# Four idle products ahead of the first large one, and the samples' heads at full width of the array

## The chip, the cores and the metric

The kernel runs on one core of a Trainium2 chip. The metric is the device time of one execution in microseconds (us). The engines are TensorE (PE; its weight loads are shown as PEld), VectorE (DVE), ScalarE (ACT), GpSimd (POOL) and SyncE (SP), which issues most DMAs. Each engine works through its own queue in order and waits on semaphores for the others.

## What is computed

The reference is one inference step of a hybrid decoder layer, for a prompt of 1024 tokens and for 8 samples of 4 tokens each, with a width of 1024. Cut to what matters here:

```
h, gate = adaln_in(x, c, w_ada, b_ada, g_norm)
(mq, mk, mv, mi, mf, mo, mz, aq, ak, av, az, gm, ga) = split_in(h @ w_in)
y_m, C, n, m = mlstm_branch(mq, mk, mv, mi, mf, mo, mz, C0, n0, m0, ...)
...                                  # windowed attention gives y_a
u = sigmoid(gm) * (y_m @ w_mo) + sigmoid(ga) * (y_a @ w_ao)
x = x + gate * (u @ w_o)             # then a last RMSNorm
```

The mLSTM branch has 4 heads of 128 channels. For the samples, a head takes its 32 tokens together:

```
s   = (q k^T) * exp(dmat - m_hat)        # 32 x 32, zero between samples
num = s v + w_inter * (q C)              # C: one 128 x 128 matrix a sample
C_new = decay * C + sum_s w_end k_s v_s^T
```

## The kernel before

Activations are kept with channels on the 128 partitions and tokens in columns. Large matrix products take each operand as a high and a low part in fp32r and add three products of the parts (h_h with wh, h_h with wl, h_l with wh). Small products and transpositions are plain f32; one of these is carried out as two passes (a transposition as one). The rows of the profile show a pass as rows * columns of the array that its weights take (128*128, 128*32, 32*32) and the size of its output.

TensorE's order is fixed by the program: `in_order` ties each product or transposition to the one before it, and `mm` and `tr` record them (L275 and L280). DVE and ACT are tied in the same way (class `Ordered`, L220) only in the first stage and the last one; from `V.on = S.on = False` on, a scheduler places their instructions by what they depend on. POOL is placed by the scheduler from the start. Every tile comes from a pool; a new tile of a tag waits until the tile whose buffer it takes over has been read for the last time. PSUM has four tags with two buffers each: `pg`, `pa`, `pb` and `po`.

**The first stage.** `warm(11)` issues eleven products of a tile of ones into a `pb` tile that nobody reads. Sums of squares of x follow as the loads of x land, then `ada_halves(adas[0])`: the first of the adaLN rows (`ada_q`), copied by ACT and turned by small products (`adat_q`) into columns in two `pb` tiles. ACT and DVE make the scales A and B from them, ACT makes h_h of the first two channel blocks, POOL casts the first weights (wh_ak, wh_av), DVE makes the low parts. The loop over `two` then runs `pair`, the large products for keys and values (`g_ak`, `g_av`), with the row sums for the second half (`xb`), more `ada_q` chunks and gate products in between.

**The middle.** `block_products` runs the input projections in pairs of 128 columns as seven block products each (Strassen's form with Winograd's sums): twelve passes of 512 columns into one of the banks bx, bw, by and bz. Between the passes `side.tick()` lets streams of smaller work issue a step: the prompt's heads (`head`, stream m), attention, weights for the last stage (`out_weights`, stream g: wor, wosh, wosl) and the samples' heads (`sample_head`, stream s). A planner's clock in the program (`side.now`) decides when a step may come; it counts product sizes and lags.

**A sample's head.** `qs`, `ks` and `vs` hold the samples' q, k and v for all heads, [128, 4, 32] each. `sample_head(h)` transposes the 32 columns of k and of v (tile stk), multiplies k and q into sS, forms `et` (a sum of `sxb` and the mask, its Exp, then times sS) and `vn` (v with a column of ones) in slices of the tile z (sz), and makes weighted copies of v (vf, vm). Its num is a sum in one bank (sn) of eight products with the samples' states, each for 32 columns at a different place (128*32), and one last product of et and vn over 32 rows (32*32). The heads' steps lie around 449, 473, 514 and 537 us in the profile; the third and fourth stand among the products of the query gates, whose `zt` is DVE's product of a gate and the attention's output.

## Time and profile before

| what | value |
|---|---|
| times of three runs | 822.41, 822.54, 823.28 us, median 822.54 |
| profiled execution, own time | 822.1 us |
| its span, first to last instruction | 820.3 us |
| mean granted TensorE clock | 0.995 |
| DMA | 165.49 MB, mean 202 GB/s |
| chain that ended last, PE's part | 19% of the span, DVE 2%, ACT 0% |

The profile's page gives busy time by engine, 40 slices of the span, DMA queues, the chain of work that ended last and the costliest groups. The chain here goes back only to 631 us. Other views answer questions on a stretch: the timeline (start, duration, engine, line, operation, tiles, shape, how many; in brackets the idle time of the engine before it and what ended that), and the windows (for each stretch its length, busy time, granted clock, DMA share and GB/s). In a timeline row of pipelined matmuls the duration is modelled and overlaps the next row, so the pace is read from one start to the next.

### The profile page before, as it was taken

To read this page: it belongs to the slowest core of one execution; us is meant where nothing else is said; L and a number is where in the kernel's file an instruction comes from. 1 tells how busy PE (TensorE), PEld (TensorE's weight loads), DVE (VectorE), ACT (ScalarE), POOL (GpSimd) and SP (SyncE) were. 2 spreads that over 40 slices of the span, in tenths; PEclk is the share of its full clock that TensorE was granted. 3 is DMA by queue.
4 is the path that set the end of the run, shared out by engine and by line. 5 is a ranking of instruction groups with operands and counts; after the bars stand their busy time and mean duration, and the time that the engine had idled before them with its cause. 6 is when DMAs were issued, how large, how long until landed. Compare 5 with 4: busy or idle time off the path is not lost. (4 is left out here: it accounts for less than half of the span.)

```text
span 820.3 us, 15125 instructions
## 1 busy us (share of the span) xinstructions
PE 805.5 (98%) x5154; PEld 667.0 (81%) x5154; DVE 603.4 (74%) x1518; ACT 419.5 (51%) x1021; POOL 49.1 (6%) x117
## 2 busy tenths in 40 slices
PE   8999999999999999999999999999999999999996
PEld 5779898888788878888888878778888779997775
DVE  5799887655755557475667889898668997876666
ACT  5664356655665564546556555554446652224334
POOL 0120000010000000000001011010002101000000
PEclk9999999999999999999999999999999999999998
DMA  9993746547545415537664675764436689647622
GB/s 353 376 333 113 251 162 214 176 148 216 176 139 162 161 56 161 162 132 259 234 213 156 234 261 189 267 210 143 146 107 205 210 302 383 220 143 278 206 104 109
DMA packets 113473, 165.49 MB, mean 202 GB/s; under 512 B 21184, under 2 KB 55744, under 8 KB 113364
## 3 DMA queue, kind: packets, MB, share of 16 engines
q1 hardware_dynamic: 107172, 152.74, 55.7%
q10 hardware_dynamic: 4752, 7.60, 2.5%
q0 software_dynamic: 1472, 4.20, 1.3%
q8 instruction: 40, 0.66, 0.3%
q14 instruction: 37, 0.30, 0.1%
HBM read 115.51 MB, written 50.00 MB: 202 GB/s over the span
## 5 line engine op out<-in xcount | busy, mean ns | idle before, releaser
L220 ACT ACTIVATE p<-p,nmx 128x256 f32<-128x256 f32 (+1 forms) x64 | 31.1, 486 | 19.5 <-DVE nmx L220 19.4
L220 DVE CUSTOM_DVE_ANT_0 p<-sc,cst,sink 128x256 f32<-128x256 f32 (+1 forms) x64 | 26.1, 462 | 9.1 <-PE sc L275 9.0
L275 PE MATMUL g_aq<-h_h,wh_aq 128*128 128x384 f32 (+1 forms) x96 | 32.3, 337 | 0.0
L275 PE MATMUL g_aq<-h_h,wl_aq 128*128 128x384 f32 (+1 forms) x96 | 30.9, 322 | 0.0
L275 PE MATMUL g_aq<-h_l,wh_aq 128*128 128x384 f32 (+1 forms) x96 | 30.9, 321 | 0.0
L275 PE MATMUL g_w_mo<-ym_l,wh_w_mo 128*128 128x384 f32 (+1 forms) x96 | 30.8, 321 | 0.0
L275 PE MATMUL g_w_mo<-ym_h,wh_w_mo 128*128 128x384 f32 (+1 forms) x96 | 30.8, 321 | 0.0
L275 PE MATMUL g_w_mo<-ym_l,wl_w_mo 128*128 128x384 f32 (+1 forms) x96 | 30.8, 321 | 0.0
L220 ACT CAST wosh<-wor 128x512 fp32r<-128x512 f32 x24 | 14.8, 621 | 12.8 <-DVE wor L220 12.8
L220 DVE COPY p<-pt 128x512 f32<-128x512 f32 (+1 forms) x16 | 10.5, 657 | 14.6 <-PE pt L280 14.6
L275 PEld LDWEIGHTS g_aq<-h_h,wh_aq 128*128 128x128 f32 x96 | 18.0, 188 | 2.6 <-issue 1.5
L261 POOL DMA_DIRECT2D oD<-uqv x16 | 8.9, 556 | 179.2 <-ACT uqv L220 163.6
L275 PE MATMUL sc<-ukv,uqv 64*128 64x256 f32 (+1 forms) x128 | 18.0, 390 | 1.0 <-DMA ukv<-kD 0.9
L220 DVE SCALAR_TENSOR_TENSOR tgw_mo<-tgw_mo,g_w_mo 128x384 f32<-128x384 f32 (+1 forms) x24 | 12.4, 518 | 8.6 <-PE g_w_mo L275 6.8
L220 DVE TENSOR_TENSOR wosl<-wor,wosh 128x512 fp32r<-128x512 f32 x24 | 16.5, 686 | 2.7 <-ACT wosh L220 2.6
L275 PEld LDWEIGHTS g_w_mo<-ym_l,wh_w_mo 128*128 128x128 f32 x96 | 18.0, 188 | 0.0
L275 PEld LDWEIGHTS g_aq<-h_l,wh_aq 128*128 128x128 f32 x96 | 18.1, 188 | 0.0
L275 PEld LDWEIGHTS g_w_mo<-ym_h,wh_w_mo 128*128 128x128 f32 x96 | 18.0, 188 | 0.0
L275 PEld LDWEIGHTS g_aq<-h_h,wl_aq 128*128 128x128 f32 x96 | 18.0, 188 | 0.0
L275 PEld LDWEIGHTS g_w_mo<-ym_l,wl_w_mo 128*128 128x128 f32 x96 | 18.0, 188 | 0.0
L220 DVE TENSOR_TENSOR et<-et,S 128x384 f32<-128x384 f32 (+1 forms) x12 | 6.1, 509 | 15.8 <-PE S L275 15.8
L275 PE MATMUL g_mq<-h_h,wh_mq 128*128 128x384 f32 (+1 forms) x48 | 16.7, 349 | 0.3 <-ACT mk L220 0.3
(2070 smaller groups left out, 2820.4 us busy)
## 6 DMA issues: line engine op xcount, KB each, us to landing
early_h<-w_ada SPq DMA_DIRECT2D x8, 512.0 KB
adar_ga<-w_ada SPq DMA_DIRECT2D x16, 256.0 KB
wr_ga<-w SPq DMA_DIRECT2D x16, 256.0 KB
wr_gm<-w SPq DMA_DIRECT2D x16, 256.0 KB
taD<-gt SPq DMA_DIRECT2D x16, 256.0 KB
tmD<-gt SPq DMA_DIRECT2D x16, 256.0 KB
wor<-w_out SPq DMA_DIRECT2D x16, 256.0 KB
tga<-taD SPq DMA_DIRECT2D x16, 256.0 KB
```

The source lines that it names most:

```text
L220: ins = f(*args, **kw)
L261: ins = (eng or nc.sync).dma_start(out, in_)
L275: in_order(nc.tensor.matmul(out, lhsT, rhs, start=start, stop=stop, skip_group_check=more))
```

## The change

Three edits, all on small products:

- behind `ada_halves(adas[0])` and ahead of the first `pair`, `warm(4)` issues four more products of the tile of ones into a `pb` tile that nobody reads;
- `qs`, `ks` and `vs` become parts of one tile `kvq` in the order k, v, q, so that four neighbouring blocks of 32 columns can be read as one operand of 128: the head's transpositions and its product for S read such a block, beginning with the head's own, and only the first 32 rows of the result are used, as before;
- the product of et and vn reads all 128 rows of z, so z[:, 128:289] is set to zero first by POOL.

```
-        qs = cp.tile([128, NH, NS], F32, name="qs")
-        ks = cp.tile([128, NH, NS], F32, name="ks")
-        vs = cp.tile([128, NH, NS], F32, name="vs")
+        kvq = cp.tile([128, 3 * NH, NS], F32, name="kvq")
+        ks, vs, qs = (kvq[:, NH * i:NH * i + NH] for i in range(3))
...
             vn, et, ns4 = z[:NS, 128:257], z[:NS, 257:289], z[:, 289:418]
+            G.memset(z[:, 128:289], 0.0)
...
-            tr(tk[:NS, 0], ks[:, h], ident)
-            tr(tk[:NS, 1], vs[:, h], ident)
+            whole = lambda i: kvq[:, i:i + 4].rearrange("p h s -> p (h s)")
+            tr(tk[:, 0], whole(h), ident)
+            tr(tk[:, 1], whole(NH + h), ident)
...
-            mm(S_[:NS], ks[:, h], qs[:, h], start=True, stop=True)
+            mm(S_, whole(h), qs[:, h], start=True, stop=True)
...
-            mm(num[:NS], et, vn, start=False, stop=True)
+            mm(num[:NS], z[:, 257:289], z[:, 128:257], start=False, stop=True)
...
         ada_halves(adas[0])
+        warm(4)
         rows[1] = pa([128, 512], "xb1")
```

The names in the rows below carry numbers that shift by a few between the two programs; the part ahead of the last number tells which tile it is. On TensorE, at the end of the first adaLN rows, the program had

```order
L275 MATMUL ada_q01_352<-early_h0_183,c32_102 32x256 x2
L275 MATMUL adat_q00_371<-cst_100,adas_q0_350 128x9 x2
L275 MATMUL adat_q01_383<-cst_100,adas_q0_350 128x9 x2
L275 MATMUL g_ak0_391<-h_h0_397,wh_ak0_0_376 128x384
L275 MATMUL g_av0_392<-h_h0_397,wh_av0_0_379 128x384
L275 MATMUL g_ak0_391<-h_h0_397,wl_ak0_0_377 128x384
```

and now has, at the same place on TensorE:

```order
L275 MATMUL ada_q01_350<-early_h0_181,c32_102 32x256 x2
L275 MATMUL adat_q00_369<-cst_100,adas_q0_348 128x9 x2
L275 MATMUL adat_q01_381<-cst_100,adas_q0_348 128x9 x2
L275 MATMUL warm_388<-one_104 128x128 x4
L275 MATMUL g_ak0_394<-h_h0_400,wh_ak0_0_374 128x384
L275 MATMUL g_av0_395<-h_h0_400,wh_av0_0_377 128x384
```

The four products stand between the last small product and the first large one; nothing else moves on TensorE, where the heads' steps keep their places.

DVE and ACT are placed by the scheduler in the middle of the program, and there some pieces change places around each sample's head. At the third head (tiles with a 2 ahead of the number: sz, stk2, sS2, vf2) DVE had this row; wl_pquery_gate0_7 is the low part of weights for a later product:

```order
L220 TENSOR_TENSOR wl_pquery_gate0_2__6404<-wr_az0_1_6090,wh_pquery_gate0_2__6403 128x512
L220 TENSOR_TENSOR wr_az0_1_6090<-wr_az0_1_6090,wr_az0_0_6088 128x512
L220 TENSOR_TENSOR skn_6332<-stk2_6342,skn_6332 32x128
L220 TENSOR_TENSOR wl_pquery_gate0_7__6439<-wr_az1_0_6092,wh_pquery_gate0_7__6438 128x512
L220 COPY sz_6331<-stk2_6342 32x128
L220 TENSOR_TENSOR sz_6331<-sxb_1794,cst_100 32x32
L220 TENSOR_TENSOR qd_6354<-qs_135,sxb_1794 128x8x4
L220 TENSOR_TENSOR vf2_6359<-sz_6331,wm_6357 32x387
L220 TENSOR_TENSOR sz_6331<-sz_6331,sS2_6350 32x32
```

and now has, on DVE at the same head:

```order
L220 TENSOR_TENSOR sz_6336<-sxb_1797,cst_100 32x32
L220 TENSOR_TENSOR wl_pquery_gate0_2__6410<-wr_az0_1_6095,wh_pquery_gate0_2__6409 128x512
L220 TENSOR_TENSOR wr_az0_1_6095<-wr_az0_1_6095,wr_az0_0_6093 128x512
L220 TENSOR_TENSOR skn_6337<-stk2_6348,skn_6337 32x128
L220 COPY sz_6336<-stk2_6348 32x128
L220 TENSOR_TENSOR sz_6336<-sz_6336,sS2_6356 32x32
L220 TENSOR_TENSOR wl_pquery_gate0_7__6445<-wr_az1_0_6097,wh_pquery_gate0_7__6444 128x512
L220 TENSOR_TENSOR qd_6360<-kvq_135,sxb_1797 128x8x4
L220 TENSOR_TENSOR vf2_6365<-sz_6336,wm_6363 32x387
```

The addition for et, the copy of the transposed v and the product with sS have gone ahead of wl_pquery_gate0_7. On ACT, a little later at the same head (wosh is a high part for the last stage, from the out_weights stream, wh_pquery_gate a high part of the query gates' weights), the row was

```order
L220 CAST wosh_6378<-wor40_5965 128x512
L220 ACTIVATE gt_6390<-by_6143 128x512
L220 COPY by_6459<-bw_6322 128x512
L220 CAST wh_pquery_gate1_1__6463<-wr_az2_0_6395 128x512
L220 CAST wosh_6418<-wor40_5965 128x512
L220 CAST wh_pquery_gate0_3__6530<-wr_az0_1_6090 128x512
L220 COPY p5_6434<-bz_6408 128x512
L220 CAST wh_pquery_gate0_4__6556<-wr_az1_1_6094 128x512
```

and now it is, on ACT:

```order
L220 CAST wosh_6384<-wor40_5970 128x512
L220 ACTIVATE gt_6396<-by_6148 128x512
L220 COPY by_6465<-bw_6327 128x512
L220 CAST wosh_6424<-wor40_5970 128x512
L220 CAST wh_pquery_gate1_1__6469<-wr_az2_0_6401 128x512
L220 COPY p5_6440<-bz_6414 128x512
L220 CAST wh_pquery_gate0_3__6536<-wr_az0_1_6095 128x512
L220 CAST wh_pquery_gate0_4__6562<-wr_az1_1_6099 128x512
```

The second wosh has gone ahead of the cast of wh_pquery_gate1_1, and the copy p5 ahead of that of wh_pquery_gate0_3. DVE's pieces for the same weights follow these in the new order.

## The prediction

> **What bounds the kernel now.** I read the page first, then the granted clock in short windows, then the timeline of each engine around the edited places.

> ```profile
> span 820.3 us, 15125 instructions
> PE 805.5 (98%) x5154; PEld 667.0 (81%) x5154; DVE 603.4 (74%) x1518; ACT 419.5 (51%) x1021; POOL 49.1 (6%) x117
> ```

> TensorE is busy for 98% of the span, so time leaves the span only where TensorE itself gets shorter, or where a wait of TensorE goes. The span is 820.3 us and the profiled execution took 822.1 us, 1.8 us around it; the median of the runs shown is 822.54 us, 0.44 above. I sum against 822.1 and add 0.44 at the end. The differences looked for are small: 0.2% is 1.65 us, about the least that a measurement of this kernel can tell from no change.

> TensorE does not run at one rate. The windows view (us from the start; TensorE busy, granted clock, DMA share, GB/s) shows one place at half clock, and a later one for comparison:

> ```profile
> 22.00:23.00 1.00, 0.09 (x1) 0.98 1.04 426
> 23.00:24.00 1.00, 0.85 (x3) 0.50 1.00 410
> ...
> 26.00:27.00 1.00, 1.00 (x10) 0.81 1.03 422
> 19.55:22.96 3.41, 2.35 (x28) 1.00 1.05 417
> 91.23:94.64 3.41, 2.48 (x20) 1.00 0.95 284
> ```

> The clock falls at 22.96 (0.98 of that microsecond) and is back at 26.38 (0.81): 3.41 us at half rate. The stretch of the same length ahead of the fall has 2.35 us of TensorE work, so 1.06 us without; 91.23 to 94.64, with 2.48, kept its clock. What TensorE does there (start, duration, what, how often):

> ```profile
> 21.03 1.06 PE L275 MATMUL adat_q<-cst,adas_q 128*128 128x9 f32 x8 [0.20 <-ACT adas_q L220]
> 23.15 0.66 PE L275 MATMUL g_ak<-h_h,wh_ak 128*128 128x384 f32 x1 [1.06 <-POOL wh_av L220]
> 23.61 0.52 PE L275 MATMUL g_av<-h_h,wh_av 128*128 128x384 f32 x1
> ...
> 25.85 1.30 PE L275 MATMUL xb<-xdg,one 128*128 128x128 f32 x8
> 26.91 0.42 PE L275 MATMUL g_ak<-h_l,wh_ak 128*128 128x384 f32 x1
> ...
> 29.64 0.44 PE L275 MATMUL g_ak<-h_h,wh_ak 128*128 128x384 f32 x1
> 29.92 0.34 PE L275 MATMUL g_av<-h_h,wh_av 128*128 128x384 f32 x1
> ```

> **The four idle products.** They stand in the hole from 22.09 (end of adat_q) to 23.15. What limits their start and what surrounds them:

> ```profile
> 21.94 0.26 ACT L220 ACTIVATE B<-adat_q,vec 128x9 f32<-128x9 f32 x1
> 22.22 0.61 POOL L220 CAST wh_av<-wr_av 128x512 fp32r<-128x512 f32 x1 [1.21 <-DMA wr_av<-w]
> 24.12 1.29 DVE L220 TENSOR_TENSOR h_l<-y,h_h 128x512 fp32r<-128x512 f32 x2
> ```

> Their tile takes over the buffer of the first adat_q tile (the pool has two, in turn), which ACT has read at 22.20. So they start at about 22.25. A 128x128 f32 product is two passes, and a pass takes 0.11 us at full clock (the tv rows below: 0.33 for three): 8 x 0.11 = 0.88, ended at 23.13, just ahead of 23.15. Behind them stands g_ak, which waits for other engines until then; I cost the products at nothing, with 0.05 us if they run over. If they start at half clock they take 1.8 us and the start would slip by 0.9.

> If the clock holds, TensorE's work from 23.15 goes at the rate of 29.64: 0.28 to the second product (29.64 to 29.92), then 0.174 each. Eight products: 0.28 + 7 x 0.174 = 1.50, so xb starts at 24.65 in place of 25.85. Its eight passes take 7 x 0.11 + 0.03 = 0.80, and g_ak<-h_l starts at 25.45 in place of 26.91: **1.45 us** earlier. The bounds are 0 (clock falls all the same) and 1.71 (half of 3.41 us). Is something else late next? The operand h_l is two DVE pieces from 24.12; the first is done at 24.77 and the second at 25.41, both in time. Then TensorE reaches the next quarter of w_ada (ada_q, at 27.79 now) at 26.35. That is 2.1 MB, queued behind wr_av, whose landing released POOL at 22.22; at 415 GB/s it is in at 27.3. The products take it in order for 1.9 us and want its last quarter at 27.8, so 0.5 us are left. TensorE waits for no DMA in this stretch now. DVE and ACT follow TensorE's adat_q there, so they move along.

> **The heads' transpositions and S.** Each of four heads (448.7, 473.4, 514.0, 537.4) has two transpositions and one two-pass product at 32 columns between large ones:

> ```profile
> 514.02 0.27 PE L280 MATMUL stk<-cst,ks 128*32 128x128 f32 x1
> ...
> 514.51 0.50 PE L275 MATMUL by<-t4h,wh_pgate__6261 128*128 128x512 f32 x1
> 514.85 0.39 PE L275 MATMUL by<-t4l,wh_pgate__6261 128*128 128x512 f32 x1
> ```

> From the first transposition to the second large product it is 0.83 us. What the same work costs at full width stands in the prompt's heads:

> ```profile
> 262.47 0.49 PE L280 MATMUL tv<-cst,hv 128*128 128x128 f32 x3
> 262.80 0.83 PE L275 MATMUL S<-hq,hk 128*128 128x128 f32 x6
> 263.39 0.48 PE L275 MATMUL by<-t4h,wh_phead_in__3296 128*128 128x512 f32 x1
> 263.70 0.39 PE L275 MATMUL by<-t4l,wh_phead_in__3296 128*128 128x512 f32 x1
> ```

> A full transposition takes 0.11, a pass of S 0.11 but the last one 0.03, and the large product behind it 0.31. So 2 x 0.11 + 0.11 + 0.03 + 0.31 = 0.67: **0.15 us less a head**. The trace has no 128*128 pass with 32 moving columns there; I take the price of the 128-column ones, the ends are 0.10 and 0.23.

> **The product of et and v.**

> ```profile
> 525.06 1.08 PE L275 MATMUL smp<-wr_az,c 128*32 128x128 f32 x32
> 525.96 0.62 PE L275 MATMUL sn<-Cs,qd 128*32 128x129 f32 x16
> 526.51 0.40 PE L275 MATMUL sn<-sz 32*32 32x129 f32 x2
> 526.84 0.50 PE L275 MATMUL by<-t3h,wh_pquery_gate__6438 128*128 128x512 f32 x1
> ```

> At 128*32, smp runs four passes side by side every 0.11 us (32 in 0.90) and goes over into sn without a break. The four groups of sn take 0.44 at that pace, but sn<-sz starts 0.55 behind them, so going to 32*32 costs 0.11; it then takes 0.33. At 128*32 two more passes take 0.11 and 0.20 (to the next form): 0.88 becomes 0.75, **0.13 us less a head**. Together 0.28 a head. The added 128x161 memset of z is POOL work (6% busy) ahead of three small copies that nothing waits for.

> **What moves on DVE and ACT.** The zeroed z makes et's first addition and its Exp stand earlier, and other pieces change places. At three heads DVE and ACT are ahead of TensorE by more than a microsecond (the shortest lead, 1.45, is quoted with the last rival), so nothing follows. At the third head they are not:

> ```profile
> 530.59 0.50 PE L275 MATMUL bx<-h_h,wh_pquery_gate__6463 128*128 128x512 f32 x1 [0.71 <-DVE zt L220]
> 517.37 0.69 DVE L220 TENSOR_TENSOR wl_pquery_gate__6439<-wr_az,wh_pquery_gate__6438 128x512 fp32r<-128x512 f32 x1 [1.23 <-ACT wh_pquery_gate__6438 L220]
> 517.98 0.27 DVE L220 COPY sz<-stk 32x128 f32<-32x128 f32 x1
> 518.85 0.17 DVE L220 TENSOR_TENSOR sz<-sz,sS 32x32 f32<-32x32 f32 x1
> 523.51 0.69 DVE L220 TENSOR_TENSOR wor<-wor,wor 128x512 f32<-128x512 f32 x1
> 525.50 0.68 DVE L220 TENSOR_TENSOR wl_pquery_gate__6531<-wr_az,wh_pquery_gate__6530 128x512 fp32r<-128x512 f32 x1
> 529.85 0.68 DVE L220 SCALAR_TENSOR_TENSOR zt<-zt,bx 128x512 f32<-128x512 f32 x1
> 523.38 0.62 ACT L220 CAST wh_pquery_gate__6463<-wr_az 128x512 fp32r<-128x512 f32 x1
> 524.24 0.62 ACT L220 CAST wosh<-wor 128x512 fp32r<-128x512 f32 x1 [0.24 <-DVE wor L220]
> 524.77 0.61 ACT L220 CAST wh_pquery_gate__6530<-wr_az 128x512 fp32r<-128x512 f32 x1
> ```

> TensorE waits here for zt, the last of a DVE row that starts with the wait at 517.37. The copy of stk, the addition and the product with sS go ahead of it, into its 1.23 us of idle time, so the row runs 0.5 us earlier and wor starts at 523.0. But ACT now does wosh ahead of the cast that stood at 523.38 and filled the time until wor was there. Wosh comes 0.73 behind wor's start (524.24 - 523.51): 523.7. Then follow the cast (524.2), the copy p<-bz (524.75) and the cast that stood at 524.77, from 525.2 to 525.85. DVE's piece of 525.50 starts at 525.87, and zt 0.37 later than now. So TensorE starts bx **0.37 us later** than before, reckoned from 512, and the third head's 0.28 are lost in that wait. From there DVE and TensorE are late together.

> **The sum:** 822.1 - 1.45 - 3 x 0.28 + 0.37 = 820.2; with the 0.44, **820.6 us**.

> **Rivals.**
> - The clock gives nothing. Four products in a hole may not be what decides, or the timed runs did not all pay the drop (their spread, 822.41 to 823.28, is less than 1.45, which speaks for all paying). Then 822.54 - 0.84 + 0.37 = 822.1. [...]
> - The third head loses nothing, since ACT's pieces fall otherwise than I laid them: 822.54 - 1.45 - 4 x 0.28 = 820.0.
> - The heads give nothing while the clock does: wider weight loads eat what the switches give: 822.54 - 1.45 = 821.1.
> - Slower: what I find at the third head happens at all four. A cast and the subtraction behind it (0.62 + 0.69 = 1.31) come late at each in place of 0.28 gained: 822.54 - 1.45 + 4 x 1.31 = 826.3. It decides once an evacuation is late by more than its slack; the shortest of the others is at the first head, where bx is free at 460.22 and taken at 461.67, 1.45 us. Against it: a single displaced piece is 0.6.

> ```profile
> 459.64 0.58 ACT L220 ACTIVATE gt<-bx 128x512 f32<-128x512 f32 x1
> 461.67 0.50 PE L275 MATMUL bx<-h_h,wh_pgate__5571 128*128 128x512 f32 x1
> ```

> **How the numbers follow.** Forecast 0.50 (820.6, itself 819.9 to 821.3), no gain by the clock 0.22 (822.1), third head harmless 0.17 (820.0), heads worth nothing 0.07 (821.1), slower 0.04 (826.3). Faster by over 0.2% means below 820.9: two thirds of the forecast's 0.50 and nearly all of the 0.17 make 0.50; the rest, 0.46, is within 0.2%; slower 0.04. The range reaches from 819.3 (clock at its upper bound, third head harmless) to 822.3, just past the case without the clock's gain.

> **What would show it.** Right: a granted clock of 1.00 in every window from 22 to 27, warm at 22.25 for about 0.9 us, xb near 24.65; 0.67 from stk to the second large product; no 32*32 rows, and 0.75 from sn to the large product behind it; the wait ahead of bx near 530 grown from 0.71 to about 1.35. Wrong: a clock of 0.50 in any stretch of 3.41 us between 15 and 30, a wait of TensorE for a DMA before 60, a stk group at 0.83 or longer, or new waits of TensorE for ACT or DVE at the first, second or fourth head.

## The result, and the profile after

The changed kernel takes **821.12 us** (median of 13 runs, 820.27 to 822.38), the kernel before, run beside it, 822.41 (13 runs, 821.06 to 823.50). The ratio is 0.9979, 95% interval 0.9971 to 0.9987: 1.3 us or 0.21% faster (1.1 to 2.4 us by the interval), with 820.6 forecast and a range of 819.3 to 822.3. The profiled execution took 821.22 us, its span is 819.4.

The head of the page after, the two lines that answer to those of before (span; busy time, share of the span and instructions of each engine):

```profile
span 819.4 us, 15145 instructions
PE 804.3 (98%) x5162; PEld 667.4 (81%) x5162; DVE 603.0 (74%) x1518; ACT 418.8 (51%) x1021; POOL 48.7 (6%) x121
```

TensorE is 1.2 us less busy and the span is 0.9 shorter. The windows view after (start and end in us; length, busy time of each engine with its instructions, granted clock, DMA share, GB/s), two windows where the clock fell before and two ahead of that:

```profile
23.00:24.00 1.00, 0.84 (x7) 0.74 (x8) 0.97 (x5) 0.97 (x3) 0.00 (x0) 1.00 1.01 414
26.00:27.00 1.00, 1.00 (x10) 1.00 (x9) 0.44 (x2) 0.00 (x0) 0.00 (x0) 1.00 1.04 426
...
10.30:13.72 3.42, 2.51 (x16) 1.31 (x18) 1.77 (x6) 1.88 (x4) 0.00 (x0) 1.00 1.07 406
13.72:17.13 3.41, 3.41 (x16) 0.80 (x8) 2.92 (x17) 1.83 (x4) 0.00 (x0) 0.50 1.03 410
```

From 22 to 27 the clock is now 1.00 throughout. But in this execution it falls **nine microseconds earlier**, at 13.72, for the same 3.41 us; the window ahead of that has 2.51 us of TensorE work. The prediction named a clock of 0.50 between 15 and 30 as a sign of being wrong, and by the letter that sign is here: the last 2.13 us of the stretch lie behind 15. TensorE's timeline after, where the products are:

```profile
22.15 1.06 PE L275 MATMUL adat_q<-cst,adas_q 128*128 128x9 f32 x8 [0.47 <-ACT adas_q L220]
23.37 1.16 PE L275 MATMUL warm<-one 128*128 128x128 f32 x8 [0.16 <-ACT B L220]
24.29 0.42 PE L275 MATMUL g_ak<-h_h,wh_ak 128*128 128x384 f32 x1
24.55 0.34 PE L275 MATMUL g_av<-h_h,wh_av 128*128 128x384 f32 x1
...
26.59 0.42 PE L275 MATMUL g_ak<-h_l,wh_ak 128*128 128x384 f32 x1
```

The eight passes hold TensorE for 0.92 us (23.37 to 24.29), and g_ak's step to g_av is 0.26 where it was 0.46 at half clock. From here on I compare by the **lead**: the start of a TensorE instruction before minus the start of the same instruction in the other kernel, each from its own span's start. g_ak<-h_l started at 26.91 and now starts at 26.59: a lead of 0.32. At adat_q it was 21.03 - 22.15 = -1.12. So the stretch won 1.44. Of the 1.12 lost ahead of it the drop at 13.72 took 0.53: the lead at 12.6 was -0.59 already.

The third head after, in TensorE's timeline (stk, S, the large products behind them; sn and what follows; the wait ahead of bx):

```profile
513.32 0.38 PE L280 MATMUL stk<-cst,kvq 128*128 128x128 f32 x2
513.53 0.31 PE L275 MATMUL sS<-kvq 128*128 128x32 f32 x2
513.67 0.48 PE L275 MATMUL by<-t4h,wh_pgate__6266 128*128 128x512 f32 x1
513.99 0.40 PE L275 MATMUL by<-t4l,wh_pgate__6266 128*128 128x512 f32 x1
...
525.12 0.62 PE L275 MATMUL sn<-Cs,qd 128*32 128x129 f32 x16
525.56 0.38 PE L275 MATMUL sn<-sz 128*32 128x129 f32 x2
525.87 0.50 PE L275 MATMUL by<-t3h,wh_pquery_gate__6444 128*128 128x512 f32 x1
...
530.19 0.50 PE L275 MATMUL bx<-h_h,wh_pquery_gate__6469 128*128 128x512 f32 x1 [1.30 <-DVE zt L220]
```

From stk to the second large product it is 0.67 us (513.32 to 513.99), 0.83 before. From sn to the next large product it is 0.75, 0.88 before. And bx waits 1.30 for zt, 0.71 before. The reason stands in ACT's and DVE's timelines after:

```profile
521.70 0.57 ACT L220 COPY by<-bw 128x512 f32<-128x512 f32 x1
523.05 0.62 ACT L220 CAST wosh<-wor 128x512 fp32r<-128x512 f32 x1 [0.78 <-DMA woDb214h<-wosh]
523.58 0.62 ACT L220 CAST wh_pquery_gate__6469<-wr_az 128x512 fp32r<-128x512 f32 x1
524.58 0.62 ACT L220 CAST wh_pquery_gate__6536<-wr_az 128x512 fp32r<-128x512 f32 x1
...
522.33 0.69 DVE L220 TENSOR_TENSOR wor<-wor,wor 128x512 f32<-128x512 f32 x1
523.70 0.69 DVE L220 TENSOR_TENSOR wosl<-wor,wosh 128x512 fp32r<-128x512 f32 x1 [0.69 <-ACT wosh L220]
525.23 0.69 DVE L220 TENSOR_TENSOR wl_pquery_gate__6537<-wr_az,wh_pquery_gate__6536 128x512 fp32r<-128x512 f32 x1 [0.23 <-ACT wh_pquery_gate__6536 L220]
529.46 0.67 DVE L220 SCALAR_TENSOR_TENSOR zt<-zt,bx 128x512 f32<-128x512 f32 x1
```

ACT is idle for 0.78 us ahead of wosh, where before a cast stood, and runs wosh 0.72 behind wor's start. (The profile names a DMA as what ended that wait; wor from DVE, at 522.33 plus its 0.69, comes at the same time, and wosh stands 0.73 behind wor's start in the kernel before too, where the profile names DVE.) DVE waits 0.69 for wosh, where before it had a piece of the query gates to do; the casts behind wosh are late as well, DVE waits 0.23 for one of them, and zt follows.

### The profile page after: what moved, and what is told of

It reads as the page before. It is cut to its first block, busy times and chain, and to the rows that moved or that the text cites. A ratio compares the mean times of both kernels' runs of the same rounds, so it can differ in the third digit from the quotient of the medians.

```text
span 819.4 us, 15145 instructions
## 1 busy us (share of the span) xinstructions
PE 804.3 (98%) x5162; PEld 667.4 (81%) x5162; DVE 603.0 (74%) x1518; ACT 418.8 (51%) x1021; POOL 48.7 (6%) x121
## 5 line engine op out<-in xcount | busy, mean ns | idle before, releaser
L220 ACT ACTIVATE p<-p,nmx 128x256 f32<-128x256 f32 (+1 forms) x64 | 31.1, 486 | 18.9 <-DVE nmx L220 17.9
L220 DVE CUSTOM_DVE_ANT_0 p<-sc,cst,sink 128x256 f32<-128x256 f32 (+1 forms) x64 | 26.1, 463 | 9.1 <-PE sc L275 9.0
L275 PE MATMUL g_aq<-h_h,wh_aq 128*128 128x384 f32 (+1 forms) x96 | 32.4, 337 | 0.1
L275 PE MATMUL g_aq<-h_h,wl_aq 128*128 128x384 f32 (+1 forms) x96 | 30.9, 322 | 0.0
L275 PE MATMUL g_aq<-h_l,wh_aq 128*128 128x384 f32 (+1 forms) x96 | 30.8, 321 | 0.0
L275 PE MATMUL g_w_mo<-ym_l,wh_w_mo 128*128 128x384 f32 (+1 forms) x96 | 30.8, 321 | 0.0
L275 PE MATMUL g_w_mo<-ym_h,wh_w_mo 128*128 128x384 f32 (+1 forms) x96 | 30.8, 321 | 0.0
L275 PE MATMUL g_w_mo<-ym_l,wl_w_mo 128*128 128x384 f32 (+1 forms) x96 | 30.8, 321 | 0.0
L220 DVE COPY p<-pt 128x512 f32<-128x512 f32 (+1 forms) x16 | 10.5, 656 | 15.2 <-PE pt L280 15.2
L220 ACT CAST wosh<-wor 128x512 fp32r<-128x512 f32 x24 | 14.8, 621 | 13.1 <-DVE wor L220 12.3
L275 PEld LDWEIGHTS g_aq<-h_h,wh_aq 128*128 128x128 f32 x96 | 18.0, 188 | 2.8 <-issue 1.5
L220 DVE TENSOR_TENSOR wosl<-wor,wosh 128x512 fp32r<-128x512 f32 x24 | 16.5, 686 | 3.9 <-ACT wosh L220 3.2
L275 PE MATMUL sc<-ukv,uqv 64*128 64x256 f32 (+1 forms) x128 | 18.0, 390 | 0.9 <-DMA ukv<-kD 0.9
L220 DVE SCALAR_TENSOR_TENSOR tgw_mo<-tgw_mo,g_w_mo 128x384 f32<-128x384 f32 (+1 forms) x24 | 12.4, 518 | 8.6 <-PE g_w_mo L275 6.4
L275 PEld LDWEIGHTS g_w_mo<-ym_l,wh_w_mo 128*128 128x128 f32 x96 | 18.0, 188 | 0.0
L275 PEld LDWEIGHTS g_aq<-h_l,wh_aq 128*128 128x128 f32 x96 | 18.1, 188 | 0.0
L275 PEld LDWEIGHTS g_w_mo<-ym_h,wh_w_mo 128*128 128x128 f32 x96 | 18.0, 188 | 0.0
L275 PEld LDWEIGHTS g_w_mo<-ym_l,wl_w_mo 128*128 128x128 f32 x96 | 18.0, 188 | 0.0
L275 PEld LDWEIGHTS g_aq<-h_h,wl_aq 128*128 128x128 f32 x96 | 18.0, 188 | 0.0
L220 DVE TENSOR_TENSOR et<-et,S 128x384 f32<-128x384 f32 (+1 forms) x12 | 6.1, 509 | 15.0 <-PE S L275 15.0
L275 PE MATMUL g_mq<-h_h,wh_mq 128*128 128x384 f32 (+1 forms) x48 | 16.7, 349 | 0.3 <-ACT mk L220 0.3
```

The lines of the kernel that those rows point to most:

```text
L220: ins = f(*args, **kw)
L275: in_order(nc.tensor.matmul(out, lhsT, rhs, start=start, stop=stop, skip_group_check=more))
```

## The experiments

All ran in three groups; the kernels of a group shared the runs of the kernel before, whose medians were 822.39 (35 runs), 822.18 (26) and 822.92 (35). Two tables from all of them stand ahead of the single runs. The first, from the traces, has the leads at places named by their time before; "wait" is that ahead of bx near 530, "half clock" the start and length of half-rate stretches ahead of 40 us.

```
kernel              21.5     27 |   440  526.6  532.8    560 | gained  wait | half clock
the change         -1.12   0.33 |  0.17   0.98   0.37   0.66 |   0.49  1.30 | 13.7 3.4
products only       0.18   1.56 |  1.34   1.34   1.35   1.35 |   0.01  0.70 | none
heads only         -0.02  -1.41 | -1.90  -1.09  -1.69  -1.42 |   0.49  1.31 | 23.9 6.8
stk and S only      0.08   1.54 |  1.79   2.20   2.19   2.35 |   0.55  0.73 | none
et and v only      -0.32  -0.44 | -0.77  -0.37  -0.99  -0.86 |  -0.09  1.28 | 24.1 3.4
late memset        -0.64   0.82 |  0.39   1.20   1.07   1.35 |   0.96  0.84 | 13.0 3.4
late, again        -0.10   1.35 | -0.41   0.40   0.27   0.55 |   0.96  0.84 | none
late, 2nd hole     -0.17   1.26 |  0.69   1.50   1.38   1.66 |   0.97  0.84 | none
2nd hole, again    -0.11   0.19 |  0.02   0.83   0.70   0.98 |   0.96  0.84 | none
two products       -0.23   1.23 |  1.20   2.01   1.43   1.70 |   0.51  1.30 | none
two, again          0.18   1.54 |  2.04   2.85   2.26   2.53 |   0.49  1.30 | none
narrow             -0.26   1.19 |  0.81   1.62   1.03   1.31 |   0.51  1.30 | none
narrow, again      -0.09   1.35 |  1.78   2.59   2.01   2.29 |   0.51  1.29 | none
```

"Gained" is from 440 to 560, the four heads. It repeats to 0.02 us between executions of kernels with the same heads, while the times of whole executions differ by 2 us and more. So the heads are judged by leads, and the clock by counts over all runs:

```
idle products       runs   mean clock 0.995 or below   median us of these   of the others
none                 130             66                     823.05             821.43
four, 128 columns     63              1                     821.20             820.49
two, 128 columns      24              8                     822.45             820.83
four, 1 column        24             11                     823.13             820.90
```

"None" is the kernel before beside the three groups (49 of 96) and the three kernels with all or parts of the heads' change and no idle products (17 of 34). By group the kernel before has 23 of 35, 12 of 26 and 14 of 35. The 63 runs with four products are of four kernels (the change, the products alone, the late memset, and that with two products more), so the medians of different rows are not to be compared; those of one row are. Profiles with a half-rate stretch near 23 show 0.994 or 0.995, those with none ahead of 40 us 0.997 or 0.998, and those with one near 13 show 0.995 and 0.996. So a run at 0.996 may have paid a drop too, and the counts are rather too low than too high. (One of the 66 is on record at 0.947 with 823.3 us; its time doesn't show so low a clock.)

Second, the work in the windows ahead of a fall. On their grids the two profiles hold 472 windows at full clock, and four are followed by half clock. TensorE's busy time alone doesn't part these from the others: one with 2.51 us lost the clock (10.30 to 13.72, after), one with 2.35 kept it (529.13 to 532.54, after). Leaving out xc (one column) and adat_q (nine columns), it does in these two profiles: the four have 0.00, 1.00 (both at the end), 1.29 (19.55 to 22.96, before) and 1.52 (10.30 to 13.72, after), and none of the others has less than 1.72 (20.54 to 23.96, after). By this reading the hole of 1.06 us cost the clock together with the 1.06 us of adat_q ahead of it. The line was drawn after the runs; no run was made to test it.

### The four products alone

```diff
         ada_halves(adas[0])
+        warm(4)
```

> The kernel before with the four idle products alone; the heads are as before. Theory (the products keep the clock, but only where the hole at 22.1 to 23.15 would have cost it; the windows of 3.41 us lie differently against the program in each execution, so an execution can pay at 13.7 instead): the clock in the profile shows no half-rate stretch that begins between 20 and 26, though one that begins at 12.5 to 14 may stand; the waits of TensorE at 530 stay 0.71; the median is 0.4 to 1.4 us below the kernel before, and the fastest runs of the two (821.1 before) lie within 0.3 of each other, as the best phase of before pays no drop either. Rival (the products do nothing on the mean, the 1.29 us came from the heads): within 0.2 us. Rival (the products give all of it): 1.3 us or more.

821.33 us (11 runs), ratio 0.999, 0.998 to 1.000. No run at 0.995 or below, where 23 of the 35 beside it were; wait near 530 unchanged; lead from 21.5 to 27 is 1.38. Its fastest run, 820.16, is not below the fastest of before, 819.80. The windows view of this kernel:

```profile
19.17:22.58 3.41, 2.93 (x36) 2.07 (x29) 3.02 (x11) 1.88 (x7) 1.07 (x2) 1.00 1.04 414
22.58:26.00 3.42, 3.42 (x26) 3.29 (x25) 3.00 (x7) 1.81 (x3) 0.15 (x1) 1.00 1.03 420
```

The fastest runs lie 0.36 apart, not within the 0.3 expected; the rest of the theory holds: the products take away a drop that about half of the executions pay, and the best executions of before seem to pay none.

### The heads alone

The changed kernel without `warm(4)`.

> The changed kernel without the four idle products. Theory: the lead over the kernel before, taken between equal TensorE instructions at 440 and at 560, grows by 0.28 at the first, second and fourth head and falls by 0.29 at the third, 0.55 in all, with the wait ahead of bx near 530 at 1.30; the profile may show a half-rate stretch that begins anywhere from 20 to 26. Median 0.3 to 0.9 us below the kernel before. Rival (heads are worth nothing, all came from the clock): lead unchanged, within 0.2 us. Rival (all came from the heads): 1.1 to 1.4 us below.

821.82 us (12 runs), ratio 0.9997, 0.9986 to 1.0008. Gained over the heads: 0.49, with the wait at 1.31. By time alone it can't be told from the kernel before, nor from the 0.3 to 0.9 expected. Its profiled execution shows what the products guard against, in the windows view:

```profile
20.44:23.85 3.41, 2.01 (x17) 1.33 (x11) 1.97 (x6) 1.98 (x5) 1.17 (x2) 1.00 1.02 415
23.85:27.27 3.42, 3.15 (x10) 2.75 (x11) 2.60 (x7) 1.52 (x2) 0.00 (x0) 0.50 1.03 422
27.27:30.68 3.41, 3.41 (x18) 2.32 (x21) 1.28 (x2) 1.46 (x3) 0.00 (x0) 0.50 1.01 408
```

Here the clock stays at half for two windows, 6.8 us: the first of them has 0.27 us without work, as TensorE waited for a DVE piece. (In the kernel before the window at half clock has 0.19 us without work, 3.23 of 3.42, and the clock came back behind it; that the wait made the second window is a reading of one profile.) The execution took 824.08 us.

### The transpositions and S alone

The kernel before with `kvq` and these lines; no memset, and et and v as before.

```diff
-            tr(tk[:NS, 0], ks[:, h], ident)
-            tr(tk[:NS, 1], vs[:, h], ident)
+            tr(tk[:, 0], whole(h), ident)
+            tr(tk[:, 1], whole(NH + h), ident)
...
-            mm(S_[:NS], ks[:, h], qs[:, h], start=True, stop=True)
+            mm(S_, whole(h), qs[:, h], start=True, stop=True)
```

> The kernel before with the samples' transpositions and S read whole, and nothing else: no memset, the product of et and v from 32 rows as before; DVE's and ACT's pieces keep their order. Theory: each stk step takes 0.15 less (0.83 becomes 0.68) at all four heads, no step at sn; and because the order is kept, the wait ahead of bx near 530 stays between 0.71 and 0.87 (what TensorE wins at the third head ahead of a DVE row that does not follow it is waited out there). Lead gained from 440 to 560: 0.45 to 0.60. Rival (the wait near 530 grows because TensorE arrives earlier, not because of the order): wait 1.1 or more and lead gained below 0.3.

822.06 us (11 runs), ratio 0.9999, 0.9988 to 1.0010: too small for the time. By leads the theory is met: 0.55 gained in four steps of 0.13 to 0.15, all kept. The wait row, and two windows of this execution:

```profile
528.39 0.50 PE L275 MATMUL bx<-h_h,wh_pquery_gate__6461 128*128 128x512 f32 x1 [0.73 <-DVE zt L220]
...
18.43:21.85 3.42, 3.06 (x42) 2.16 (x41) 2.92 (x12) 1.58 (x5) 1.32 (x2) 1.00 1.05 412
21.85:25.26 3.41, 2.35 (x17) 2.24 (x17) 3.19 (x8) 2.51 (x5) 0.00 (x0) 1.00 1.02 416
```

With DVE's and ACT's order kept, the wait stays at 0.73. The windows tell as much: the hole of 1.06 us is there, unfilled (21.85 to 25.26 has 2.35 us of work), and the **clock does not fall**. In the profile of before the window with 2.35 us of work lost it. There the other work was adat_q, of 9 columns, and ada_q, at 128*32; here most of it is products of 128x384 at 128*128. Without adat_q the window of before has 1.29 us, and the one here, where only 0.17 us of adat_q falls in, has 2.19.

### The product of et and v alone

The kernel before with these two lines.

```diff
+            G.memset(z[:, 128:289], 0.0)
...
-            mm(num[:NS], et, vn, start=False, stop=True)
+            mm(num[:NS], z[:, 257:289], z[:, 128:257], start=False, stop=True)
```

> The kernel before with the memset of z and the product of et and v from 128 rows, and nothing else; the transpositions and S are as before. DVE's and ACT's pieces stand as in the changed kernel. Theory: each sn step takes 0.13 less, but the order at the third head delays zt: the wait ahead of bx near 530 is 1.1 to 1.3 and the lead falls there by 0.35 to 0.6, so that from 440 to 560 the lead changes by -0.2 to +0.15: this part of the change is worth nothing as it stands. Rival (the order does no harm): wait within 0.71 to 0.85, lead gained 0.39 to 0.52.

822.09 us (11 runs), ratio 0.9999, 0.9987 to 1.0011. Four steps of 0.11 to 0.13, and a loss of 0.62 at the third head's wait (just beyond the 0.35 to 0.6 expected): -0.09 in all. This half of the heads' change is worth nothing as it stands. The wait in this kernel:

```profile
531.55 0.50 PE L275 MATMUL bx<-h_h,wh_pquery_gate__6466 128*128 128x512 f32 x1 [1.28 <-DVE zt L220]
```

### The memset issued later

The changed kernel; the same work, one line moved.

```diff
             vn, et, ns4 = z[:NS, 128:257], z[:NS, 257:289], z[:, 289:418]
-            G.memset(z[:, 128:289], 0.0)
...
             tr(tk[:, 1], whole(NH + h), ident)
+            G.memset(z[:, 128:289], 0.0)
```

> The changed kernel with the memset of z issued four statements later, behind the two transpositions; it computes the same, and DVE's and ACT's pieces stand again as in the kernel before at all four heads. Theory (the third head loses because of the order): the wait ahead of bx near 530 is 0.8 to 1.0 in place of 1.30 (0.71 and what the two steps of that head gain ahead of a DVE row that does not follow them), and the lead over the kernel before, between equal TensorE instructions from 440 to 560, grows by 0.7 to 1.0 in place of 0.48. Rival (the wait grows because TensorE arrives earlier): 1.2 to 1.3 as before, lead 0.45 to 0.6. The mean granted clock of all runs is 0.996 or above, as in the 24 runs with the four products so far. Median 1.3 to 2.0 us below the kernel before.

> The kernel with the late memset of z and the four products once more, beside the next one, since 7 runs each did not part the two. Theory: mean granted clock 0.996 or above in at least 9 of 10 runs, median 1.5 to 2.5 us below the kernel before; the wait ahead of bx near 530 again 0.84 in whatever execution is profiled.

819.78 us (7 runs) and 819.87 (12 runs), **both ratios 0.9967, 0.9955 to 0.9979**. The wait is 0.84 and 0.96 is gained over the heads, in both profiles. Wait, ACT's row and zt in the first of them:

```profile
529.51 0.50 PE L275 MATMUL bx<-h_h,wh_pquery_gate__6469 128*128 128x512 f32 x1 [0.84 <-DVE zt L220]
...
521.82 0.57 ACT L220 COPY by<-bw 128x512 f32<-128x512 f32 x1
522.30 0.62 ACT L220 CAST wh_pquery_gate__6469<-wr_az 128x512 fp32r<-128x512 f32 x1
523.16 0.62 ACT L220 CAST wosh<-wor 128x512 fp32r<-128x512 f32 x1 [0.24 <-DVE wor L220]
...
528.78 0.68 DVE L220 SCALAR_TENSOR_TENSOR zt<-zt,bx 128x512 f32<-128x512 f32 x1
```

The cast stands ahead of wosh again and fills the time until wor is there. The wait exceeds that of before by 0.13, the step of sn in this head: DVE's row doesn't follow it. So the loss at the third head is the order's, 0.47 us, and one statement's place decides it. This version beats both kernels. Its gain in the medians, 2.7 us by the ratio (822.2 x 0.0033), is more than the leads and the clock account for (0.96 and, below, 0.74); the interval reaches down to 1.7. Both medians lie further below the kernel before (2.4 and 3.05 us) than expected; what the rest is, if it is there, no run told. One expectation failed: not all runs were at 0.996 or above. The first profiled execution, at 0.995, has a drop at 12.96, ahead of the four products and out of their reach:

```profile
9.54:12.96 3.42, 2.52 (x13) 1.09 (x10) 1.90 (x4) 1.58 (x4) 0.00 (x0) 1.00 1.04 390
```

### Two more products in the earlier hole

The late memset, and two products where TensorE waits for xsum.

```diff
+        warm(2)
         x_cols(xc0, 0)
```

> As the run with the late memset, and two more idle products in the earlier hole of 0.68 us, in which TensorE waits for xsum at 11.8 to 12.5. Theory: no half-rate stretch can begin near 13.7 either (one of the profiles with the four products alone had one); TensorE is not late at 12.5, as the two products take 0.44. Median 0 to 0.4 us below the run with the late memset, 1.5 to 2.2 below the kernel before. Rival (the products delay the column sums or the xs row behind them): xc starts later than xsum is ready, 0.2 us or more lost at 14.

> Late memset, four products, and the two products in the hole of 11.8 to 12.5, once more. If the earlier hole costs on the mean (two of three profiles without a drop at 23 had one near 13, at 0.6 to 1.1 us): median 0.2 to 0.6 us below the run beside it. If what is gained there is waited out later (654 and 744, where TensorE waited for DVE in most profiles): within 0.2 us.

(The drop near 13.7 that the first of these names is the changed kernel's; the profile with the four products alone has none.) 819.99 us (8 runs), ratio 0.9973, 0.9960 to 0.9986, and 820.66 (12 runs), 0.9979, 0.9968 to 0.9991. All 20 runs were at 0.997 or 0.998, and neither profile has a drop near 13, yet the time is not lower than with the late memset alone: 820.50 for the 20 runs, 819.82 for the 19, so neither forecast of a lower median was met, nor the second's other case, within 0.2 us. The products delay nothing where they stand, in the first of the two:

```profile
11.18 0.71 PE L275 MATMUL warm<-one 128*128 128x128 f32 x4
11.93 1.05 PE L275 MATMUL xc<-cst,xsum 128*128 128x1 f32 x8
```

xc starts no later than it did (the lead at 12.6 is -0.03, -0.12 in the first profile with the late memset). A drop near 13 costs 0.5 (the lead after goes from -0.59 at 12.6 to -1.12 at 18), and only some executions pay it. Part of what is won there was lost later: between 632 and 656, TensorE's wait for wl_ao1A alone was 0.94 in the first profile. In the second the loads were late, with the clock at full rate (TensorE and POOL):

```profile
23.54 0.34 PE L275 MATMUL g_av<-h_h,wh_av 128*128 128x384 f32 x1
24.86 0.44 PE L275 MATMUL g_av<-h_h,wl_av 128*128 128x384 f32 x1 [0.52 <-DVE wl_av L220]
...
22.15 0.61 POOL L220 CAST wh_ak<-wr_ak 128x512 fp32r<-128x512 f32 x1 [20.95 <-DMA wr_ak<-w]
```

POOL's cast of wr_ak started at 20.43 in the repeat with the late memset, here at 22.15. Whether that was chance, or the two products cost something, stays open; they are no gain.

### Two products in place of four

`warm(2)` for `warm(4)`, all else as changed.

> The changed kernel with two idle products in place of four: 0.44 us, so that 0.6 of the hole's 1.06 us stay idle. [...] Rival (the hole has to be filled whole): 0.995 or below in a third of the runs or more.

> Two products in place of four, once more: 5 of 12 runs were at 0.995 or below, though the profiled one was not. Theory (what is left idle still loses the clock where a window of 3.41 us has the whole hole and the narrow products ahead of it): 0.995 or below in a quarter to a half of the runs; a profile of such a run shows the half-rate stretch beginning between 22.5 and 24.5. Rival (the five were chance, or fell elsewhere): at most one, or a stretch that begins near 13.

821.11 us (12 runs), ratio 0.9987, 0.9978 to 0.9997, and 821.06 (12 runs), 0.9987, 0.9975 to 1.0000. Of the first I expected at least 10 of 11 runs at 0.996 or above, and was wrong: 7 of 12 were, and 5 and then 3 runs were at 0.995 or below, 8 of 24. Half a hole still costs a third of the executions their clock, as the second expectation had it; where their half-rate stretch began stays unshown. Neither profiled execution was one of these; in the first the window that the products stand in has 3.00 us of work:

```profile
20.21:23.63 3.42, 3.00 (x28) 2.07 (x25) 3.31 (x11) 2.43 (x6) 1.22 (x2) 1.00 1.04 417
```

### Four products of one column

```diff
-        def warm(n):
+        def warm(n, m=128):
...
-                mm(w, one, one, start=True, stop=True)
+                mm(w[:, :m], one, one[:, :m], start=True, stop=True)
...
-        warm(4)
+        warm(4, 1)
```

> The changed kernel with four idle products of one moving column each in place of 128 (the same weights; 8 passes at about 0.12 us, as those of xc with xsum, fill about the same time). Theory A (idleness decides: TensorE is occupied, by weights too): the clock holds as with 128 columns, 0.996 or above in all but one run. Theory B (the rows streamed decide, since xc's and adat_q's narrow products stand in the windows that lost the clock): 0.995 or below in a third of the runs or more, median 0.5 to 1.0 us above the changed kernel.

> Four products of one moving column, once more: 4 of 12 runs were at 0.995 or below, two of these at 0.990 and 5 us longer. Theory (rows streamed decide, not occupation): 0.995 or below in a quarter to a half again; a profile of such a run has the hole filled (idle under 0.3 in the window ahead) and a half-rate stretch behind it all the same. Rival (occupation decides): at most one in ten.

821.34 us (12 runs), ratio 0.9996, 0.9980 to 1.0013, and 822.27 (12 runs), 1.0001, 0.9987 to 1.0015: by time the gain of the whole change is gone, though the heads' 0.5 us still stand in the leads. 4 and 7 runs were at 0.995 or below, 11 of 24, as often as with no products. And the products do fill the hole (the repeat):

```profile
22.35 1.05 PE L275 MATMUL warm<-one 128*128 128x1 f32 x8 [0.16 <-ACT B L220]
23.26 0.42 PE L275 MATMUL g_ak<-h_h,wh_ak 128*128 128x384 f32 x1
...
22.07:25.48 3.41, 3.25 (x25) 3.14 (x25) 3.19 (x8) 2.46 (x5) 0.62 (x1) 1.00 1.02 419
```

The eight passes hold TensorE for 0.91 us, where those of 128 columns hold it for 0.92, with one column streamed each. So by the counts, in this hole, **occupying TensorE with one-column passes didn't hold the clock (11 of 24 runs at 0.995 or below); passes of 128 columns did (1 of 63)**. What isn't shown is where the half-rate stretch fell in the 11 runs: the two profiled executions had none. Their windows end at 22.09 and 22.07, close to the 21.85 of the transpositions and S alone, which kept the clock with the hole empty; so they say nothing on windows that end where the clock was lost, at 22.96 (before) to 24.1 (et and v alone).

## Why the prediction was right, and where it wasn't

- **The clock, its size: right.** 1.45 us was forecast from 21.5 to 27, and 1.36 to 1.46 was measured wherever the clock held and the loads were in time. The DMA's half microsecond of slack was enough: no new wait of TensorE for w_ada appeared, also where TensorE came 1.5 us earlier (the products alone).
- **The clock, how often: wrong.** The step that failed is the spread of the timed runs, "less than 1.45, which speaks for all paying". Three runs were too few. Without products 66 of 130 runs were at 0.995 or below, so the term is worth about 1.45 x 66/130 = 0.74 on the mean, not 1.45 (0.58 to 0.95 by the shares of the single groups). The medians of the two sorts, 823.05 and 821.43, are 1.62 apart, about the forecast's 1.45 for one execution.
- **Why only half: the windows.** In five profiles drops began at 13.0, 13.7, 23.0, 23.9 and 24.1 and lasted 3.4 us or twice that, so they lie differently against the program in each execution; before and after, the early fall stands 232 and 235 times 3.413 us ahead of the last. That the place of the grid decides whether an execution pays is my reading: the counts show how many do, but no run shows where the grid lay in an execution without a profile. The window ahead of a fall can be empty: with the change no product runs from 811.59 on, and the clock falls at 815.85. It need not be: windows with 2.01 to 2.52 us of TensorE's work lost it too (20.44 to 23.85 with the heads alone, 9.54 to 12.96 with the late memset).
- **The hole of 1.06 us as the cause: half right.** It is not the idle time alone. A window with 2.35 us of work lost the clock among narrow products (19.55 to 22.96, before) and kept it among wide ones (21.85 to 25.26, stk and S alone), and with one-column products in the hole 11 of 24 runs were at 0.995 or below, with none 66 of 130. The prediction took the hole for the cause and had no term for adat_q, which fills its eight passes with nine columns each.
- **The transpositions and S, 0.15 a head: right.** 0.67 was forecast for 0.83 and is there to the hundredth; the leads grow by 0.13 to 0.15.
- **The product of et and v, 0.13 a head: right.** 0.75 was forecast and measured.
- **The third head, bx 0.37 later: right.** The wait was forecast at "about 1.35" and measured at 1.30; the four heads together at 3 x 0.28 - 0.37 = 0.47, and measured at 0.49. The mechanism, wosh ahead of the cast on ACT, was tested by moving the memset alone: the order went back at all four heads, and the wait to 0.84.
- **The memset at nothing: right for its time, not for its place.** Its 0.47 us are not POOL's work; it stood where it made the order of DVE and ACT change. The prediction priced that at the third head and didn't see that the line could stand elsewhere.
- **The sum.** Heads 0.49 and clock 0.74 make 1.23; 1.29 was measured, 1.94 forecast from 822.54. The gain came out 0.65 short, and the clock's frequency accounts for 0.71 of that. That 1.23 and 1.29 lie so close is partly luck: the interval of the measured gain is 1.1 to 2.4 us, and the share of executions that pay differs between the groups. The lower end of the range, 819.3, leaves out the 0.44 that the forecast adds (822.54 - 1.71 - 1.12 = 819.7); the measured 821.12 is above both.
- **The rivals.** No gain by the clock: 1 of 63 runs against 66 of 130 speaks against it, though its second ground, that not all runs pay the drop, was true. The third head harmless: no, but true once the memset is moved. Heads worth nothing: no. Lateness at all four heads: no wait of TensorE appeared at the first, second or fourth head.

## What to carry to other kernels

A drop of TensorE's clock that one profile shows is a draw: count the mean granted clock over many runs before pricing it (66 of 130 were low here), and fill a hole with products of many columns: in this one four of 128 columns left 1 of 63 runs at 0.995 or below, four of one column 11 of 24. Small gains on the engine that sets the time are read from the starts of equal instructions, which repeated to 0.02 us, when whole runs differ by 2. Where a scheduler places the work, the place of one cheap statement can cost more than the statement's purpose gains (et and v alone: four steps of 0.11 to 0.13 us gained, 0.62 lost at the third head): compare the order of the other engines, and try the line a few statements later.

## What the runs showed that was not expected

One wait for a load moved by nearly as much as the whole change between two executions. The wait for ukv at 92 us, in the kernel before and in the repeat with the late memset:

```profile
92.47 0.93 PE L275 MATMUL sc<-ukv,uqv 64*128 64x128 f32 x8 [0.93 <-DMA ukv<-kD]
```

```profile
92.89 0.93 PE L275 MATMUL sc<-ukv,uqv 64*128 64x128 f32 x8 [2.20 <-DMA ukv<-kD]
```

It was 0.9 in the profiled execution of before and 2.2 in one of a kernel that doesn't touch that place. Besides this, the drop of two windows with the heads alone and the failure of the one-column products, both told above, had not been expected.
